# A planner that sums three engines, gate columns as steps of their own, and projection stores from ScalarE's queue

## The chip, the cores and the metric

One core of a Trainium2 chip. The kernel is a program for its engines: TensorE (PE, with its weight loads as PEld), VectorE (DVE), ScalarE (ACT), GpSimd (POOL) and SyncE (SP), each of which works through its own instruction queue in order and waits there for semaphores of the others. The metric is the device time of one execution in microseconds (us); the smaller, the better.

## The reference, cut to what matters

One layer of a transformer trunk over 1024 latent tokens and 256 context tokens, 1024 channels, float32: a SwiGLU block, then token mixing, then another SwiGLU block. The change is within token mixing.

```python
def token_mixing(h_lat, h_ctx, w_in, ...):
    p_lat = jnp.split(h_lat @ w_in, IN_SPLITS, axis=-1)   # retention q k v gate, GLA q k v gate, two low-rank gate inputs
    p_ctx = jnp.split(h_ctx @ w_in, IN_SPLITS, axis=-1)
    ret_lat = retention_inputs(p_lat, n_lat)              # q, k with rotary embedding; 4 heads of 128
    gla_lat_f, gla_lat_b = gla_inputs(p_lat, ...)         # g = log_sigmoid(p[8] @ w_f + b_f) / 16; 4 heads, dk 64, dv 128
    o_ret_l, _ = bidir_prefix(retention_chunked, ...)     # forward and backward scans over chunks of 128,
    o_gla_l, _ = bidir_prefix(gla_chunked, ...)           # and of 64, from the context's final states
    return merge_outputs(o_ret_l, o_gla_l, p_lat, ...)    # normalise, multiply by silu(gate), @ w_out
...
def gla_chunked(q, k, v, g, s0):                          # one chunk
    b = jnp.cumsum(gc, axis=-2)
    scores = jnp.einsum('bhid,bhjd,bhijd->bhij', qc, kc, jnp.exp(b_i - b_j))
    o = scores @ vc + (qc * jnp.exp(b)) @ s
    s = jnp.exp(b_last) * s + (kc * jnp.exp(b_last - b)).T @ vc
```

## The kernel before

The whole trunk is one program: the first SwiGLU block fills the first 845 us, the context's projections follow, mixing of the latent tokens (`lat_phase`) runs from about 926 to 1431 us, `mixed_in` and `mixed_out` (the product with w_out) until about 1527 us, and the second SwiGLU block to the end. Every large product is made of three float32r matmuls (`mm3`, L67 to L69): weights and activations are split into a high part (`whi`, `hh`; ScalarE, L62) and the rest (`wlo`, `hl`; VectorE or GpSimd, L63). Latent tokens come in two halves of 512, `tg` 0 and 1.

Mixing consists of projections and of lanes that use them. A projection unit (`unit`, `unit_v`, `unit_v0`) takes its weights in pieces, accumulates in a PSUM tile `psa` (four buffers) over 8 channel blocks, and ends in `put`: ScalarE copies the tile to `pv`, and the store to a DRAM buffer (`gqd`, `gkd`, `rqd`, `rkd`, `rvd`, `gvd`, `sgd`) is issued on `self.store`, which is GpSimd's queue. The lanes load from there again, on SyncE's queue. `unit_v0` makes the first GLA values and, in 32 more columns, the low-rank gate inputs of both directions; it copies those to four tiles `p89` (L1393), transposes them on PE (L1403) and copies the result to `p89T` (L1405).

The lanes are generators, each made of steps that begin with matmuls:

- `gate_lane`: for each `tg` and head, `gla_gates`: a matmul of `p89T` with the gate weights, softplus on ScalarE (`softplus`, L814 to L818), sums over pairs, fours and so on up to 128 on GpSimd (L1089), two exponentials on ScalarE (L1091, L1092), two stores. After the four heads of `tg` 0 come `decays` (L1068), tables for retention.
- `gla_lane`, one head after another: loads, and for each level hs = 1, 2, 4, 8, 16 copies to `zq`, `zk` (L1131 to L1134), products with gate factors (L1128, L1144), score matmuls (L1153); then states, outputs, norm (`pow_half`, L1047 and L1048) and `finish` (a transpose, L1033, the gate from `sgd`, the store to `mixd`).
- `ret_lane`, one head after another: rotary products (L1265 to L1267) over tiles `rope`, `rq`, `rs` of one buffer each, states, scores, norm (L1359), `finish`.
- a lane of the context's states, whose last product is L981 for retention (`ctx_ret`) and L956 for GLA (`ctx_gla`).

Only PE's instructions are put in order by hand: `lat_phase` runs inside `pe_order`, and the order in which the generators are advanced is PE's order. The other engines' orders come from the scheduler of the programming layer. `lat_phase` keeps a clock `self.now` of PE's planned time. Each step of a lane yields the time at which its inputs should be ready, its cost on PE and the names it needs; a step whose time has come is taken, otherwise a piece of projection from `lat_units` (in the order of the list `UNITS`) fills PE. Ready times come from one counter: `vec(us)` adds 1.25 times a duration to `self.dve`, the planned time of VectorE. ScalarE and GpSimd have no counter; their work is in constants such as `+ 6`.

In the profile's names, buffer numbers are left out: `psa` and `psb` are PSUM tiles of projections and of lanes, `t` and `t2` general tiles, `sc` and `L` the gates' tiles.

Of the kernel before, what the change touches and what calls it, by code (L numbers as in the profile page):

```python
# [30 lines left out]
class Trunk:  # L31
# [899 lines left out]
    def ctx_gla(self, h, pool):  # L931
# [15 lines left out]
        yield self.vec(3) + 5, 0.44, ()  # L947
# [5 lines left out]
        yield self.now + 2, 0.44, ()  # L953
# [6 lines left out]
        self.done[f"S{h}"] = self.now  # L960

    def ctx_ret(self, h, pool):
# [15 lines left out]
        yield self.vec(0.8) + 0.8, 0.9, ()  # L978
# [6 lines left out]
        self.done[f"T{h}"] = self.now  # L985
# [43 lines left out]
    def finish(self, on, tg, wcol, hb, pool):  # L1029
# [5 lines left out]
        if hb in self.gated:  # L1035
            sg = self.tile(pool, [P, 512], F32, "sg", 2)
            nc.sync.dma_start(sg, self.sgd[hb * P:(hb + 1) * P, tg * 512:(tg + 1) * 512])
            nc.vector.scalar_tensor_tensor(out=mx, in0=pt, scalar=wcol, in1=sg, op0=ALU.mult, op1=ALU.mult)
        else:
            self.late.add((hb, tg))  # L1040
            nc.scalar.activation(mx, pt, AF.Copy, scale=wcol)
        self.store.dma_start(self.mixd[hb * P:(hb + 1) * P, tg * 512:(tg + 1) * 512], mx)
# [19 lines left out]
    def decays(self, h, pool):  # L1062
# [10 lines left out]
        self.done[f"D{h}"] = self.vec(0.6) + 4  # L1073
# [22 lines left out]
    def vec(self, us):  # L1096
        self.dve = max(self.dve, self.now) + SLACK * us
        return self.dve

    def gla_lane(self, h, pool):  # L1100
# [18 lines left out]
        def copies(hs, tg):  # L1119
# [4 lines left out]
            w = 0.8  # L1124
            if hs == 1:
# [4 lines left out]
                w = 1.5  # L1130
# [4 lines left out]
            return self.vec(w) + 0.9  # L1135

        def scale(hs, tg):
# [8 lines left out]
            return self.vec(0.46) + 1.2  # L1146

        def scores(hs, tg):
# [7 lines left out]
            elif hs == 1:  # L1156
                sc[tg] = g[tg]
                nc.scalar.copy(sc[tg], ps)
            else:
                nc.vector.copy_predicated(c3(sc[tg]), self.msk[hs].unsqueeze(1).to_broadcast([P, 4, P]), c3(ps))  # L1160
                self.vec(0.75)

        yield self.now + 4, 0, ()
        at = {0: copies(1, 0)}
        scale(1, 0)
        for hs in (1, 2, 4, 8, 16):
# [7 lines left out]
            else:  # L1174
                at[0] = self.dve + 1.2
                at[1] = max(at[1], at[0])
            yield at[1], 0.9, ()
            scores(hs, 1)
        for hs in (32, 64):
# [14 lines left out]
        for tg in LATTG:  # L1194
# [4 lines left out]
            at[tg] = self.vec(1.1) + 0.8  # L1199
            kt.append(kh)  # L1200
        for tg in LATTG:
# [7 lines left out]
            at[tg] = self.now + 2.2  # L1209
# [12 lines left out]
        last = self.vec(4.9) + 1  # L1222
        ons = []
        for tg in LATTG:
# [16 lines left out]
            ons.append((self.vec(0.8) + 4.5, on))  # L1241
# [4 lines left out]
    def ret_lane(self, h, pool):  # L1246
# [7 lines left out]
        at = {}  # L1254
        for tg in LATTG:
# [3 lines left out]
            for src, out in ((self.rkd, k), (self.rqd, q)):  # L1259
                raw, sw = self.tile(pool, [P, 512], F32, "rq", 1), self.tile(pool, [P, 512], F32, "rs", 1)  # L1260
# [3 lines left out]
                t = self.tile(pool, [P, 512], F32, "qk", 4)  # L1264
                nc.vector.tensor_tensor(out=t, in0=raw, in1=rope[:, 0, :], op=ALU.mult)  # L1265
                nc.vector.tensor_tensor(out=sw, in0=sw, in1=rope[:, 1, :], op=ALU.mult)
                nc.vector.tensor_tensor(out=t, in0=t, in1=sw, op=ALU.add)  # L1267
                out.append(t)
                at[tg] = self.vec(2.1) + 4 + 3 * tg
# [7 lines left out]
        def decayed(d, tg):  # L1277
# [3 lines left out]
            return vd, self.vec(0.5) + 0.3  # L1281

        kt = []
        for tg in LATTG:
# [7 lines left out]
            at[tg] = self.now + 2  # L1292
        parts = ((0, 0), (1, 1), (0, 1), (1, 0))
        nxt = decayed(0, 0)
        for i, (d, tg) in enumerate(parts):
# [15 lines left out]
            last = self.vec(1.4)  # L1311
# [10 lines left out]
        def decay(tg, ps):  # L1322
# [7 lines left out]
            return self.vec(2.2) + 0.6, sc, qf  # L1330

        yield self.now, 0.9, ()
        ps = inner(0)
        ready, sc, qf = decay(0, ps)
        yield self.now, 0.9, ()
        ps = inner(1)
        for tg in LATTG:
# [15 lines left out]
            self.vec(1.5)  # L1353
# [7 lines left out]
            ons.append((self.vec(1) + 3 - 2 * (tg == 0), on))  # L1361
# [4 lines left out]
    def put(self, pool, ps, dst, fn=AF.Copy, scale=1.0, view=None):  # L1366
        t = self.tile(pool, [P, 512], F32, "pv", 4)
        self.nc.scalar.activation(t, ps, fn, scale=scale)
        self.store.dma_start(dst, view(t) if view else t)
# [10 lines left out]
    def unit_v0(self, pool, w, tg):  # L1380
# [6 lines left out]
        pT = self.psB()  # L1387
        if tg == 0:
            self.pt89 = self.tile(pool, [64, 512], F32, "p89T", 1)
        rs = []  # L1390
        for c in range(4):
            r = self.tile(pool, [P, 32], F32, "p89", 4)
            nc.scalar.copy(r, ps[c][:, 256:288])  # L1393
            rs.append(r)
# [524 lines left out]
```

## Time and profile before

| what | value |
|---|---|
| median of 3 runs | 2191.18 us (2186.52 to 2196.46) |
| profiled execution, its own time | 2184.12 us |
| its span, first to last instruction | 2180.9 us |
| mean granted TensorE clock | 0.989 |
| projections' stores on GpSimd's queue, 930 to 1450 us (L1369, L1400) | 56 |
| DMA to landing for them, median | 3.3 us |
| PE busy, 1000 to 1050 us, of 50 | 47.46 us |
| PE busy, 1150 to 1200 us, of 50 | 50.00 us |

A wait in the tables reads "engine, tile and line that waits <- engine, tile and line it waited for: us in total, times, longest". In a timeline, a row's first number is the start in us from the span's start, the second the duration, and square brackets hold the idle time before it and what ended it. ACTq, POOLq and SPq are the queues of those engines, where DMAs are issued. PEclk is the clock that PE was granted, as a share of full speed.

### The profile page before, as it was taken

To read this page: it belongs to the slowest core of one execution; us is meant where nothing else is said; L and a number is where in the kernel's file an instruction comes from. 1 tells how busy PE (TensorE), PEld (TensorE's weight loads), DVE (VectorE), ACT (ScalarE), POOL (GpSimd) and SP (SyncE) were. 2 spreads that over 40 slices of the span, in tenths; PEclk is the share of its full clock that TensorE was granted. 3 is DMA by queue.
4 is the path that set the end of the run, shared out by engine and by line. 5 is a ranking of instruction groups with operands and counts; after the bars stand their busy time and mean duration, and the time that the engine had idled before them with its cause. 6 is when DMAs were issued, how large, how long until landed. Compare 5 with 4: busy or idle time off the path is not lost.

```text
span 2180.9 us, 33346 instructions
## 1 busy us (share of the span) xinstructions
PE 2119.4 (97%) x11558; PEld 1817.0 (83%) x11558; DVE 1529.7 (70%) x2735; ACT 948.6 (43%) x1776; POOL 420.5 (19%) x572
## 2 busy tenths in 40 slices
PE   8999999999999999978999999999999999999998
PEld 7888888888888999966889789878878888887888
DVE  7889999756777657745666556477777666675676
ACT  4434334345544555655332432244343433434553
POOL 0101111110013662545232322100001111120000
PEclk9999999999999999989999999999999999999999
DMA  8267768569865566655462353573134444467674
GB/s 330 83 231 245 270 221 277 178 237 308 295 196 162 174 182 201 181 194 187 148 177 83 112 173 118 178 251 98 63 128 159 140 157 159 155 218 242 208 237 153
DMA packets 209529, 409.57 MB, mean 188 GB/s; under 512 B 26128, under 2 KB 48080, under 8 KB 209360
## 3 DMA queue, kind: packets, MB, share of 16 engines
q1 hardware_dynamic: 185600, 330.77, 48.3%
q0 software_dynamic: 23328, 76.55, 8.8%
q8 instruction: 90, 1.47, 0.3%
q14 instruction: 79, 0.65, 0.1%
q10 hardware_dynamic: 432, 0.13, 0.0%
HBM read 320.56 MB, written 86.79 MB: 187 GB/s over the span
## 4 chain that ended last, share of the span: by engine, by line
PE 79%; DVE 6%; issue 5%; DMA 4%; POOL 2%; ACT 2%; SPq 0%; POOLq 0%; ACTq 0%; DVEq 0%
PE psa L67 14%; PE psa L69 14%; PE psa L68 14%; PE psb L67 10%; PE psb L69 9%; PE psb L68 9%; PE psa L1421 3%; PE psb L1153 2%; DVE hl L226 1%; POOL L L1089 1%; DVE nt L220 1%; DMA qk<-sgd 1%; DMA raw<-in_w 1%; PE psb L1301 1%; POOL rr L1048 0%
## 5 line engine op out<-in xcount | busy, mean ns | idle before, releaser
L62 ACT ACTIVATE whi<-raw 128x512 fp32r<-128x512 f32 (+1 forms) x635 | 390.7, 622 | 673.2 <-PE psa L68 212.6
L63 DVE TENSOR_TENSOR wlo<-raw,whi 128x512 fp32r<-128x512 f32 (+1 forms) x533 | 368.2, 694 | 251.6 <-ACT whi L62 244.1
L67 PE MATMUL psa<-hh,whi 128*128 128x512 f32 (+1 forms) x1444 | 535.8, 371 | 2.2 <-ACT hh L62 1.1
L69 PE MATMUL psa<-hh,wlo 128*128 128x512 f32 (+1 forms) x1444 | 528.9, 366 | 3.1 <-POOL wlo L63 3.1
L68 PE MATMUL psa<-hl,whi 128*128 128x512 f32 (+1 forms) x1444 | 528.3, 366 | 1.2 <-DVE hl L63 1.2
L67 PEld LDWEIGHTS psa<-hh,whi 128*128 128x128 f32 x1444 | 275.4, 191 | 47.1 <-ACT hh L62 1.9
L69 PEld LDWEIGHTS psa<-hh,wlo 128*128 128x128 f32 x1444 | 274.2, 190 | 48.0 <-POOL wlo L63 4.1
L68 PEld LDWEIGHTS psa<-hl,whi 128*128 128x128 f32 x1444 | 275.0, 190 | 43.4 <-DVE hl L63 2.2
L67 PE MATMUL psb<-hh,whi 128*128 128x512 f32 (+1 forms) x680 | 259.6, 382 | 0.5 <-ACT whi L62 0.5
L69 PE MATMUL psb<-hh,wlo 128*128 128x512 f32 (+1 forms) x680 | 259.5, 382 | 0.6 <-DVE wlo L63 0.6
L68 PE MATMUL psb<-hl,whi 128*128 128x512 f32 (+1 forms) x680 | 259.4, 382 | 0.0
L63 POOL TENSOR_TENSOR wlo<-raw,whi 128x512 fp32r<-128x512 f32 (+1 forms) x102 | 136.8, 1359 | 204.2 <-ACT whi L62 199.2
L353 POOL DMA_DIRECT2D gd<-s x154 | 83.7, 544 | 388.7 <-DVE s L344 298.0
L69 PEld LDWEIGHTS psb<-hh,wlo 128*128 128x128 f32 x680 | 127.8, 188 | 25.7 <-DVE wlo L63 1.0
L67 PEld LDWEIGHTS psb<-hh,whi 128*128 128x128 f32 x680 | 127.8, 188 | 25.5 <-ACT whi L62 1.0
L68 PEld LDWEIGHTS psb<-hl,whi 128*128 128x128 f32 x680 | 127.8, 188 | 24.6
L1048 POOL TENSOR_TENSOR nr<-nr,mhalf 128x4 f32<-128x4 f32 (+1 forms) x11 | 10.3, 932 | 423.1 <-DVE nr L1047 413.5
L130 DVE CUSTOM_DVE_ANT_0 junk<-ada,condc,cols 128x1024 bf16<-128x1024 f32 x62 | 79.3, 1278 | 5.0 <-DMA ada<-in_adaT 4.7
L385 POOL DMA_DIRECT2D sd<-s x22 | 11.9, 541 | 359.3 <-DVE s L384 359.2
L63 DVE TENSOR_TENSOR hl<-raw,hh 128x512 fp32r<-128x512 f32 x93 | 65.3, 709 | 9.9 <-ACT hh L62 9.8
L62 ACT ACTIVATE hh<-raw 128x512 fp32r<-128x512 f32 x93 | 57.0, 620 | 12.2 <-DMA raw<-gd 9.8
L352 DVE TENSOR_TENSOR s<-s,s 128x512 f32<-128x512 f32 x88 | 59.0, 685 | 0.4
(421 smaller groups left out, 4070.2 us busy)
## 6 DMA issues: line engine op xcount, KB each, us to landing
raw<-in_w SPq DMA_DIRECT2D x374, 256.0 KB, 3.1
gd<-s POOLq DMA_DIRECT2D x154, 256.0 KB, 3.1
ada<-in_adaT SPq DMA_DIRECT2D x76, 512.0 KB, 4.4
raw<-gd SPq DMA_DIRECT2D x88, 256.0 KB, 3.2
s<-in_w SPq DMA_DIRECT2D x66, 256.0 KB, 4.7
sd<-s POOLq DMA_DIRECT2D x44, 256.0 KB, 2.8
raw<-sd SPq DMA_DIRECT2D x44, 256.0 KB, 3.0
hh<-in_w SPq DMA_DIRECT2D x44, 256.0 KB, 3.9
```

Of the source, the lines that this page charges most:

```text
L62: nc.scalar.activation(hi, src, AF.Copy)
L63: (eng or nc.vector).tensor_tensor(out=lo, in0=src, in1=hi.bitcast(F32), op=ALU.subtract)
L67: mm(ps, wa[0], xa[0], start=start, stop=False, skip_group_check=more)
L68: mm(ps, wa[0], xa[1], start=False, stop=False, skip_group_check=more)
L69: mm(ps, wa[1], xa[0], start=False, stop=stop, skip_group_check=more)
L130: nc.vector.tensor_tensor_reduce(out=self.junk, in0=t, in1=self.cs[s], scale=1.0, scalar=self.col("ada_b")[:, j:j + 1], op0=ALU.mult, op1= ...
L220: nc.vector.scalar_tensor_tensor(out=t, in0=self.x[tg][k], scalar=a[:, k:k + 1], in1=rb, op0=ALU.mult, op1=ALU.mult)
L226: self.nc.vector.scalar_tensor_tensor(out=lo, in0=t, scalar=b[:, k:k + 1], in1=hi.bitcast(F32), op0=ALU.add, op1=ALU.subtract)
L352: sub = lambda o, a, b: nc.vector.tensor_tensor(out=o, in0=a, in1=b, op=ALU.subtract)
L353: put = lambda i, t: self.store.dma_start(self.gd[i, f // 2], t)
L1153: nc.tensor.matmul(ps[:, s], kl[:, s], ql[:, s], start=True, stop=True)
L1421: mm(o, x[p], y[q], start=k == 0 and n == 0 and c % 2 == 0, stop=k == KD - 1 and n == 2, skip_group_check=True)
```

## The change

1. `vec` and its one counter become `w(eng, us, after)` with three: `self.clk` holds planned times of VectorE (v), ScalarE (a) and GpSimd (p), with factors 1.2, 1.1 and 1.15; every ready time gets 0.7 us (`LAG`) on top. The lanes' steps charge what they put on each engine. Weight loads charge ScalarE 0.63 and VectorE 0.69 each, for the split.
2. The transposes of the low-rank columns and the copy to `p89T` move from `unit_v0` to `gate_lane`, as a step for each `tg` (L1062 and L1064 in the new numbering). The gates' steps are no longer ready all at once but one after another by ScalarE's counter, and `decays` come after both halves' gates, one step for each head.
3. `put` and `unit_v0` issue their 56 stores on ScalarE's queue (L1396 and L1426) instead of GpSimd's.
4. `rq` and `rs` get two buffers each.
5. `UNITS`: the key, query and value projections of retention heads 2 and 3 come earlier, the retention gates rg0 and rg1 later.

```diff
+    def w(self, eng, us, after=0):
+        c = max(self.clk[eng], self.now)
+        self.clk[eng] = c + SLACK[eng] * us
+        return max(c, after) + SLACK[eng] * us + 0.15
-    def vec(self, us):
-        self.dve = max(self.dve, self.now) + SLACK * us
-        return self.dve
...
     def gate_lane(self, pool):
         nc = self.nc
+        self.pt89 = self.tile(pool, [64, 512], F32, "p89T", 1)
         for tg in LATTG:
             yield 0, 0, (("ga0", "gv0")[tg],)
+            yield self.w("a", 0.8), 0.4, ()
+            pT = self.psB()
+            for c in range(4):
+                nc.tensor.transpose(pT[:32, c * P:(c + 1) * P], self.r89[c], self.ident)
+            self.p89T[tg] = self.pt89[32 * tg:32 * tg + 32]
+            nc.scalar.copy(self.p89T[tg], pT[:32])
+            at = self.w("a", 0.6)
             for h in range(4):
-                yield self.now, 0.45, ()
+                yield at, 0.45, ()
                 self.gla_gates(h, tg, pool)
-                self.done[f"G{tg}{h}"] = self.vec(1.4) + 6
-            if tg == 0:
-                for h in range(4):
-                    self.decays(h, pool)
+                t = self.w("v", 1.43, self.w("a", 1.9))
+                t = self.w("a", 1.25, self.w("p", 3.2, t))
+                at = self.clk["a"] - 2.5
+                self.done[f"G{tg}{h}"] = self.w("p", 1.2, t)
+        for h in range(4):
+            yield self.clk["a"], 0, ()
+            self.decays(h, pool)
+            self.done[f"D{h}"] = self.w("p", 0.6, self.w("v", 0.6, self.w("a", 1.6)))
...
             for src, out in ((self.rkd, k), (self.rqd, q)):
-                raw, sw = self.tile(pool, [P, 512], F32, "rq", 1), self.tile(pool, [P, 512], F32, "rs", 1)
+                raw, sw = self.tile(pool, [P, 512], F32, "rq", 2), self.tile(pool, [P, 512], F32, "rs", 2)
...
-            ons.append((self.vec(0.8) + 4.5, on))
+            t = self.w("v", 0.2, self.w("v", 0.7, self.w("a", 0.62)))
+            ons.append((self.w("a", 1.15, self.w("p", 1.3, t)), on))
...
     def put(self, pool, ps, dst, fn=AF.Copy, scale=1.0, view=None):
         t = self.tile(pool, [P, 512], F32, "pv", 4)
         self.nc.scalar.activation(t, ps, fn, scale=scale)
-        self.store.dma_start(dst, view(t) if view else t)
+        self.nc.scalar.dma_start(dst, view(t) if view else t)
+        self.w("a", 1.0)
...
         for c in range(2):
             r0 = 512 * tg + 256 * c
-            self.store.dma_start(self.gvd[r0:r0 + 256, :256].rearrange("(c p) e -> p c e", p=P), t[c].rearrange("p (c e) -> p c e", c=2))
-        yield KD, None, 0.5
-        for c in range(4):
-            nc.tensor.transpose(pT[:32, c * P:(c + 1) * P], rs[c], self.ident)
-        self.p89T[tg] = self.pt89[32 * tg:32 * tg + 32]
-        nc.scalar.copy(self.p89T[tg], pT[:32])
+            nc.scalar.dma_start(self.gvd[r0:r0 + 256, :256].rearrange("(c p) e -> p c e", p=P), t[c].rearrange("p (c e) -> p c e", c=2))
...
                 u[2].append(self.load_half(s))
+                self.w("a", 0.63), self.w("v", 0.69)
...
-                lane[1:] = y
+                lane[1:] = [y[0] + LAG, *y[1:]]
...
-UNITS = ("gv0", "gk0", "gq0", "rk0", "rq0", "rv0", "rk1", "rq1", "gk1", "gq1", "gv1", "gg0", "rg0", "gg1", "rk2", "rq2", "rv1",
-         "rg1", "rk3", "rq3", "gg2", "rg2", "gg3", "rg3")
+UNITS = ("gv0", "gk0", "gq0", "rk0", "rq0", "rv0", "rk1", "rq1", "gk1", "gq1", "gv1", "gg0", "rk2", "rq2", "rv1", "rg0", "gg1",
+         "rk3", "rq3", "rg1", "gg2", "rg2", "gg3", "rg3")
```

What it moves, at three places. First PE, at the end of the second half of gv0 (matmuls of 128x288), before: the four transposes follow at once, then the first projection of gk0 (`hh_2061`).

```order
L67 MATMUL psa_10172<-whi_10257,hh_1333_5979 128x288
L68 MATMUL psa_10172<-wlo_10258,hh_1333_5979 128x288
L69 MATMUL psa_10172<-whi_10257,hl_1334_5980 128x288
L1403 MATMUL psb_10484<-ident_82,p_2369_10485 32x128
L1403 MATMUL psb_10484<-ident_82,p_2370_10487 32x128
L1403 MATMUL psb_10484<-ident_82,p_2371_10489 32x128
L1403 MATMUL psb_10484<-ident_82,p_2372_10491 32x128
L67 MATMUL psa_10506<-hh_2061_9175,whi_10422 128x512
```

And after: the first projection follows at once; it takes the PSUM buffer that psa_10163 held.

```order
L68 MATMUL psa_10165<-wlo_10252,hh_1333_5979 128x288
L69 MATMUL psa_10165<-whi_10251,hl_1334_5980 128x288
L67 MATMUL psa_10166<-whi_10251,hh_1333_5979 128x288
L68 MATMUL psa_10166<-wlo_10252,hh_1333_5979 128x288
L69 MATMUL psa_10166<-whi_10251,hl_1334_5980 128x288
L67 MATMUL psa_10412<-hh_2061_9175,whi_10269 128x512
L68 MATMUL psa_10412<-hl_2062_9176,whi_10269 128x512
```

The transposes now stand 77 rows further on, between two projections:

```order
L68 MATMUL psa_10548<-hl_2076_9190,whi_10415 128x512
L69 MATMUL psa_10548<-hh_2075_9189,wlo_10416 128x512
L1062 MATMUL psb_10599<-ident_82,p_2352_10396 32x128
L1062 MATMUL psb_10599<-ident_82,p_2353_10398 32x128
L1062 MATMUL psb_10599<-ident_82,p_2354_10400 32x128
L1062 MATMUL psb_10599<-ident_82,p_2355_10402 32x128
L67 MATMUL psa_10598<-hh_1319_5965,whi_10346 128x512
L68 MATMUL psa_10598<-hl_1320_5966,whi_10346 128x512
```

ScalarE at the same place, before: the exponentials of the first half's gates (`sc`, `L`) and the decay tables (`dec`, `t` from `tab`) stand ahead of the copies of the low-rank columns (`p`) and of the values (`pv`) of the second half.

```order
L1092 ACTIVATE L_10320<-L_10320 128x508
L1091 ACTIVATE sc_10354<-sc_10354 128x512
L1068 ACTIVATE dec_10378<-tab_9877,lgx_9879 128x128 x3
L972 COPY t_2360_10429<-psb_10426 128x256
L1393 COPY p_2369_10485<-psa_10169 128x32
L1393 COPY p_2370_10487<-psa_10170 128x32
L1393 COPY p_2371_10489<-psa_10171 128x32
L1393 COPY p_2372_10491<-psa_10172 128x32
L1397 COPY pv_10493<-psa_10169 128x256
L1397 COPY pv_10493<-psa_10170 128x256
L1397 COPY pv_10494<-psa_10171 128x256
```

And after, with what each row waits for (DMAHW are completion semaphores that SyncE's loads use too): gates 0 and 1 stand among the copies, the decay tables are gone, and the first of gv0's stores is issued here.

```order
L1106 ACTIVATE sc_10318<-sc_10318 128x512 [waits Pool_49]
L817 ACTIVATE t_2349_10361<-t_2349_10361 128x512 [waits Activation_49]
L1418 COPY p_2353_10398<-psa_10164 128x32
L1418 COPY p_2354_10400<-psa_10165 128x32
L818 ACTIVATE t_2349_10361<-t_2349_10361 128x512 [waits Activation_49]
L1107 ACTIVATE L_10307<-L_10307 128x508 [waits Pool_49]
L1418 COPY p_2355_10402<-psa_10166 128x32
L1422 COPY pv_10404<-psa_10163 128x256
L1422 COPY pv_10404<-psa_10164 128x256
L1422 COPY pv_10405<-psa_10165 128x256
L1422 COPY pv_10405<-psa_10166 128x256
L1426 DMA gvd<-pv_10404 128x2x256 [waits DMAHW1_49,Activation_49]
```

Only one gate's last exponential (L1107) is left ahead of the value copies that free the projections' PSUM buffers.

VectorE in the GLA lane's last head before, where the second half's first level is made (`zq_2249`, `zk_2250`): the rotary product of retention's third head is in front, on its second rope tile.

```order
L63 TENSOR_TENSOR wlo_13807<-raw_13804,whi_13806 128x512
L1133 COPY zk_2250_9955<-B_2859_13516 64x256
L1265 TENSOR_TENSOR qk_13663<-rq_13656,rope_13654 128x512
L1128 TENSOR_TENSOR A_2858_13515<-A_2858_13515,sc_13511 64x512
L1131 COPY zq_2249_9954<-A_2858_13515 64x256
L1144 TENSOR_TENSOR A_2858_13515<-A_2858_13515,sc_13511 128x256
L1266 TENSOR_TENSOR rs_13657<-rs_13657,rope_13654 128x512
```

After, at the same point of the GLA lane's third head, the rotary product reads retention's first rope tile of that head:

```order
L1149 COPY zk_2250_9955<-B_2777_12931 64x256
L1288 TENSOR_TENSOR qk_13250<-rq_13243,rope_13241 128x512
L1144 TENSOR_TENSOR A_2776_12930<-A_2776_12930,sc_12926 64x512
L1147 COPY zq_2249_9954<-A_2776_12930 64x256
L63 TENSOR_TENSOR wlo_13176<-raw_13173,whi_13175 128x512
```

And for the second head, retention's second rope tile is read between the first level and the next:

```order
L1147 COPY zq_2249_9954<-A_2635_11986 64x256
L1288 TENSOR_TENSOR qk_12063<-rq_12056,rope_12054 128x512
L1161 TENSOR_TENSOR A_2635_11986<-A_2635_11986,sc_11982 128x256
L1149 COPY zk_2254_9963<-B_2636_11987 64x64x4
L1147 COPY zq_2251_9958<-A_2635_11986 64x128x2
```

The row moved from one level's copies to another's, and from the fourth head to the second and third.

More of the change, by code (lines that the diff above doesn't have):

```diff
@@ L952, in ctx_gla @@
         nc.scalar.copy(kt[:, :n], pt[:, :n])
-        yield self.now + 2, 0.44, ()
+        yield self.w("a", 0.4), 0.44, ()
         ps = self.psB()
@@ L1208, in gla_lane @@
             nc.scalar.copy(A[tg][b], B[tg][b])
-            at[tg] = self.now + 2.2
+            at[tg] = self.w("a", 0.62)
+            self.w("a", 0.4)
         for tg in LATTG:
@@ L1254, in ret_lane @@
         at = {}
+        tq = self.now + 4.5
         for tg in LATTG:
@@ L1291, in ret_lane @@
             kt.append(t)
-            at[tg] = self.now + 2
+            at[tg] = self.w("a", 0.62)
         parts = ((0, 0), (1, 1), (0, 1), (1, 0))
@@ L1329, in decay @@
             nc.vector.tensor_tensor(out=c3(sc), in0=c3(ps), in1=dec[:, 0:1, :].to_broadcast([P, 4, P]), op=ALU.mult)
-            return self.vec(2.2) + 0.6, sc, qf
-        yield self.now, 0.9, ()
+            return self.w("v", 2.25, max(last, q_at)), sc, qf
+        q_at = tq - 0.5
+        yield q_at - 3, 0.9, ()
         ps = inner(0)
         ready, sc, qf = decay(0, ps)
-        yield self.now, 0.9, ()
+        yield q_at, 0.9, ()
         ps = inner(1)
```

72 lines of the change are left out of this document (40 added, 32 removed).

## The prediction

> **What bounds the kernel now.** I read the page first: busy shares, granted clock.
>
> ```profile
> PE 2119.4 (97%) x11558; PEld 1817.0 (83%) x11558; DVE 1529.7 (70%) x2735; ACT 948.6 (43%) x1776; POOL 420.5 (19%) x572
> PEclk9999999999999999989999999999999999999999
> ```
>
> TensorE (PE) is the bound, and nearly full over the span. The change touches only mixing, 930 to 1450 us, so I then asked for the busy time there, stretch by stretch (columns: stretch, length, busy of each engine, granted clock, DMA).
>
> ```profile
> 930.00:1000.00 70.00, 53.45 (x264) 42.50 (x263) 34.77 (x89) 43.93 (x105) 36.08 (x81) 0.87 0.59 197
> ...
> 1200.00:1250.00 50.00, 47.13 (x328) 39.86 (x328) 24.48 (x48) 22.63 (x50) 17.67 (x24) 0.97 0.35 115
> 1250.00:1300.00 50.00, 45.02 (x281) 40.34 (x277) 27.30 (x60) 20.93 (x46) 14.87 (x18) 0.93 0.58 177
> ...
> sum 597.00, PE 563.20 PEld 487.36 DVE 353.52 ACT 244.75 POOL 156.01; mean PE 51.20 PEld 44.30 DVE 32.14 ACT 22.25 POOL 14.18
> ```
>
> PE is idle for 597.0 - 563.2 = 33.8 us between 930 and 1527, half of it before 1000 (70.00 - 53.45 = 16.6). Which waits these are is in PE's wait table of 930 to 1480:
>
> ```profile
> PE psb L1403 <- ACT p L1393: 12.0, 2, 11.5
> PE psb L1153 <- DVE zq L1131: 4.5, 1, 4.5
> PE psb L981 <- ACT t L818: 3.9, 1, 3.9
> PE psb L1033 <- ACT t L1240: 3.8, 3, 2.9
> PE psb L1033 <- DVE t2r L1359: 2.1, 2, 1.5
> PE psb L950 <- DVE t L946: 1.9, 1, 1.9
> PE psb L1214 <- ACT t L1207: 1.4, 2, 1.0
> ...
> PE psa L67 <- ACT hh L62: 0.7, 1, 0.7
> ```
>
> Four waits make up most of it. Each also costs afterwards: PE windows cut at the stalls show the clock.
>
> ```profile
> 971.30:975.10 3.80, 3.77 (x11) 0.50 0.59 243
> ...
> 996.20:1000.20 4.00, 3.99 (x9) 0.50 0.65 221
> 1000.20:1005.00 4.80, 4.80 (x18) 0.76 0.82 259
> ...
> 1208.00:1214.00 6.00, 6.00 (x22) 0.78 0.34 134
> ...
> 1293.40:1300.00 6.60, 6.60 (x33) 0.54 0.60 197
> ```
>
> Time lost to the lower clock is length x (1 - clock): 1.9 us after the first stall, 2.0 + 1.2 after the one at 996, 1.3 after 1207, 3.0 after 1293: 9.4 in all. So the most that any order could win in this stage is 33.8 + 9.4 = 43 us, 2% of the span.
>
> **The change, part by part.**
>
> *Low-rank transposes and gates as steps of their own.* Why the 11.5 us exist is in ScalarE's timeline:
>
> ```profile
> 950.07 0.69 ACT L814 ACTIVATE t<-psb,cols 128x512 f32<-128x512 f32 x1
> ...
> 957.74 0.63 ACT L1092 ACTIVATE L<-L 128x508 f32<-128x508 f32 x1 [1.72 <-POOL L L1089]
> ...
> 963.06 0.63 ACT L1092 ACTIVATE L<-L 128x508 f32<-128x508 f32 x1 [1.71 <-POOL L L1089]
> ...
> 968.87 0.63 ACT L1092 ACTIVATE L<-L 128x508 f32<-128x508 f32 x1 [1.19 <-POOL L L1089]
> ...
> 971.09 0.44 ACT L1393 COPY p<-psa 128x32 f32<-128x32 f32 x4
> 971.40 0.95 ACT L1397 COPY pv<-psa 128x256 f32<-128x256 f32 x3
> ```
>
> ```profile
> 959.49 0.29 PE L69 MATMUL psa<-whi,hl 128*128 128x288 f32 x1
> 971.33 1.03 PE L1403 MATMUL psb<-ident,p 128*32 128x128 f32 x4 [11.54 <-ACT p L1393]
> ```
>
> PE ends the second half of gv0 and wants its four low-rank copies at once; ScalarE serves in order and has the first half's four gates in front, whose L1092 wait each time for GpSimd's running sums. Changed, PE has other matmuls where the transposes stood, and one whole gate, no longer three and more, is ahead of the copies. It does not go to nothing: the next matmul of a projection needs the PSUM tile that these copies release, and ScalarE has L1107 (the former L1092) of gate 0 in front of it. One gate takes ScalarE from 950.07 to 957.74 + 0.63, some 8 us; the gate's matmul now stands 24 matmuls of 0.13 us (the spacing at 959) before the piece's end, 3.1 us. So 8 - 3 = 5 us stay, 6.5 of 11.5 are won. Bounds: 0 (three gates still ahead in effect) and 11.5. I count no clock gain there: 5 us idle is more than the 2.9 us at 1207 that already lowered the clock.
>
> On that clock the Trainium skill, page "TensorE: Matmul & The Clock Gate", section "HAM oscillation — how this bites in real kernels", says that only idle gaps above about 3.4 us let the clock fall. Here the 0.78 after a wait of 2.87 us differs from it; by the page the stall at 1207 costs 1.3 us less and the sum below is about 1 us smaller. I go by the row.
>
> *The context key states (L981, at 996).* Its PE wait of 3.9 plus 3.2 of clock, 7.1 us, comes from a key copy (L972) that ScalarE reaches only behind two L1092 of the second half's gates, in the same way. With gates spaced, one is ahead: I take 5 of 7.1 (bounds 0 and 7.1). A cost comes with it: the first of these products now comes earlier, behind a split of a weight that has only just landed at 946.4,
>
> ```profile
> 946.38 0.63 ACT L62 ACTIVATE whi<-raw 128x512 fp32r<-128x512 f32 x1 [1.99 <-DMA raw<-in_wgk]
> 949.28 0.63 ACT L62 ACTIVATE whi<-raw 128x512 fp32r<-128x512 f32 x1 [2.26 <-DMA raw<-in_wgk]
> ```
>
> and I charge 2.5 us, about one such wait. Net 2.5.
>
> *Rotary rows (1293).* PE waited for zq, and VectorE had stood at the rotary product:
>
> ```profile
> 1291.63 0.69 DVE L1265 TENSOR_TENSOR qk<-rq,rope 128x512 f32<-128x512 f32 x1 [4.68 <-DMA rope<-in_rope]
> 1292.24 0.68 DVE L1128 TENSOR_TENSOR A<-A,sc 64x512 f32<-64x512 f32 x1
> 1292.95 0.28 DVE L1131 COPY zq<-A 64x256 f32<-64x256 f32 x1
> ```
>
> 4.5 + 3.0 of clock. rq and rs get a second buffer, rope does not. In the new order the product that stands like this one, right ahead of GLA head 2's second-half copies, reads a rope tile whose load is issued long before; but for head 1 the second rope tile, reloaded into the one buffer, is read ahead of the next level's copies (the order of VectorE shows it). Of 7.5 I take 4 (bounds 0, 7.5).
>
> *L1033 behind L1240 (1207)*: 2.9 + 1.3 of clock; the GpSimd power of the norm is now in the plan (1.3 us) and the finish stands later. I take 2.5 of 4.2. *L1033 behind L1359* (2.1 in two): 1. *The end*: behind the last finish there now stand some 17 us of projection matmuls before w_out, where it was the last thing, so w_out's first splits,
>
> ```profile
> 1436.71 0.50 PE L67 MATMUL psa<-hh,whi 128*128 128x512 f32 x1 [0.72 <-ACT hh L62]
> 1437.85 0.50 PE L68 MATMUL psa<-hl,whi 128*128 128x512 f32 x1 [0.64 <-DVE hl L63]
> ```
>
> lose 1.4, of which I take 1. The L950 and L1214 rows (3.3) keep their causes: 0.
>
> *Stores from ScalarE's queue.* 52 stores of put and 4 of unit_v0 leave GpSimd:
>
> ```profile
> L1369 POOL DMA_DIRECT2D sgd<-pv x16: 540/581/597, 1213.9 to 1431.3; - x16
> L1369 POOL DMA_DIRECT2D rvd<-pv x8: 725/733/765, 1065.4 to 1313.7; - x8
> L1400 POOL DMA_DIRECT2D gvd<-pv x4: 715/737/782, 939.8 to 974.8; - x4
> ```
>
> ```profile
> 1.16 0.46 ACTq L76 DMA_DIRECT2D ccol<-in_ccol  x1
> ```
>
> GpSimd gives up 40 x 0.58 + 16 x 0.74 = 35 us of issuing, and stops holding its sums and rr behind a late copy. It is 19% busy and the terms above hold what PE saw of it, so further gain 0 (bounds 0 and 35). ScalarE, 244.75 of 597 us busy here, gains 56 x 0.45 = 25 us, and each store now stands in front of the next split or copy. In the order's waits it also takes turns with SyncE's loads on the same eight completion semaphores (DMAHW0 to 7), so a store can wait in ScalarE's queue for an older load, and a load for an older store. Bounds: 0 (all under ScalarE's idle) to 25 for the issues alone. In PE's table the longest wait for a projection (psa) is 0.7 us, so I am near the lower end: 3 us, one issue in eight. The Trainium skill, page "DMA: Bandwidth & Descriptors", section "Issuing engines are not separate DMA queues", speaks against any gain here: the transfers run on the same 16 DMA engines whoever issues them, and only the issuing sequencer's time is saved. By it alone this part is 0 or a loss, as I have it; no row of before shows a data store issued by ScalarE.
>
> *Decay tables after both gate halves, UNITS' new order, loads charged in the plan*: the same instructions (PE has the same number); ScalarE's L1068 leave the place before the copies, which is in the first term. Retention heads 1 to 3 start earlier, and GLA units later: hidden under fill, 0.
>
> Sum: 6.5 + 2.5 + 4 + 2.5 + 1 + 1 - 3 = 14.5 us. The profiled execution took 2184.1 (span 2180.9 and 3.2 around it), 7 below the median 2191.2 of the runs; against it the change gives 2169.6, and against the median 2191.2 - 14.5 = 2177.
>
> **Rivals.** (a) *The waits move*: PE has still eight gates to pass, each 8 us on ScalarE with two waits for GpSimd, and projections need ScalarE's copies between. If each gate costs PE 1.5 us through a PSUM tile that is released late, 12 us come back: 2189. For it: GpSimd's sums are no faster. Against it: 12 to 24 projection matmuls stand between two gates now, where four gates stood next to each other. (b) *ScalarE's queue becomes the bound* (slower): stores wait there for loads' semaphores, splits come late, PE waits on whi. A store's landing took 3.3 us in the median:
>
> ```profile
> DMA to landing us min/median/max: 2.3/3.3/6.3
> ```
>
> If PE loses 0.31 us for each of the 56, the gain of 17.5 is gone, and from there it is slower; at 0.6, 34 us, the kernel is at 2191 + 34 - 17.5 = 2207. For it, SyncE is often held, and a load that is late then holds a store, and the splits behind the store:
>
> ```profile
> SPq L264 <- DVE wlo L63: 102.2, 27, 11.3
> ```
>
> Against it, ScalarE is idle over half of the stage. (c) *Most of the stalls go*: 43 less 8 that keep their causes: 35 us, 2156. For it: every large wait has an edit aimed at its queue; against it: the 5 us worked out above.
>
> **How the numbers follow.** 0.5% is 11 us, about what a measurement of this kernel tells from no change. The forecast, terms partly won: 0.52, its own range 2166 to 2185, of which 0.39 lies below 2180 and 0.13 above. (c) 0.13, all faster. (a) 0.20: 0.02 faster, 0.17 same, 0.01 slower. (b) 0.15: 0.03 same, 0.12 slower. Together faster 0.54, same 0.33, slower 0.13. The range leaves out the far half of (c) and of (b): 2154 to 2198.
>
> **What would show it.** L1062 (the former L1403) without a wait above 1 us; one wait of about 5 us at 955 to 962 on an L67 of psa released by ACT pv, half clock after it; L982 once at 2 to 3 us near 946; no wait of 4 us near 1290; GpSimd with 56 instructions fewer; PE idle over 930 to 1527 near 20 us rather than 34. Wrong it is if PE's table gets rows of psa for ACT whi or pv above 5 us together, if ScalarE's stores wait for semaphores of loads, or if rope's wait comes back at another head with the same 4 us.

## The result, and the profile after

The changed kernel takes 2163.7 us (2162.2 to 2166.0), the kernel before 2189.2 in the same comparison: ratio 0.9879, 95% interval [0.9852, 0.9906], some 26 us faster. The direction and the stage of the forecast held, and so did the mechanism for PE's order; its size did not, 14.5 us against about 26, and one term, the stores, had the wrong sign. Both profiled executions lie at the low end of their kernel's runs, before's further than after's: they are 22 us apart (2184.1 and 2162.2), and the readings below explain those 22.

The gain is all in mixing. From the first 288-column matmul to the norm behind w_out, PE windows of before and of after, in this order (stretch, length, PE busy, granted clock, DMA):

```profile
898.10:1481.80 583.70, 548.09 (x3631) 0.97 0.51 163
```

```profile
900.50:1460.50 560.00, 539.12 (x3632) 0.99 0.53 170
```

583.7 has become 560.0 us, 23.7 less, with the same matmuls. The code ahead of this stretch and behind it is the same; it took 2.4 and 0.8 us longer in this execution of after. Idle time fell from 35.6 to 20.9, which is 14.7 of the 23.7. The other 9.0 are busy time, most of it slow matmuls that are gone. PE windows over the stretches in which the clock was at half, before and then after:

```profile
951.30:954.70 3.40, 3.40 (x14) 0.50 0.38 128
964.90:975.20 10.30, 3.87 (x12) 0.50 0.43 175
995.60:1002.50 6.90, 6.29 (x14) 0.51 0.61 207
1132.20:1135.60 3.40, 3.40 (x9) 0.50 1.04 321
1207.30:1210.70 3.40, 3.40 (x10) 0.50 0.21 78
1292.60:1299.40 6.80, 6.02 (x29) 0.50 0.56 186
```

```profile
963.30:970.20 6.90, 4.23 (x10) 0.51 0.53 190
1035.00:1038.40 3.40, 3.40 (x18) 0.50 0.72 224
1284.20:1287.60 3.40, 3.40 (x14) 0.50 0.19 77
```

PE was busy at half clock for 26.4 us before and for 11.0 after; half of each is lost, 13.2 and 5.5, so 7.7 of the 9.0 are the clock's. It added half as much again to the idle time that was won.

PE's waits of after, 920 to 1480 us:

```profile
PE psa L67 <- ACT pv L1422: 6.4, 3, 5.1
PE psb L1034 <- ACT t L1261: 4.2, 2, 3.5
PE psa L1442 <- ACT pv L1395: 2.0, 1, 2.0
PE psb L1171 <- DVE zk L1149: 1.7, 1, 1.7
PE psa L68 <- DVE hl L63: 1.4, 1, 1.4
```

No row is left of the transposes, of the context's states (L982, the former L981), of zq behind VectorE, or of L1386 (the former L1359). The one wait that the forecast kept is there, 5.09 us against 5 worked out. ScalarE's timeline has gate 0's last exponential ahead of the copies, PE's has the wait, and PE's windows show the slow clock behind it and behind the wait of 3.5 us at 1283:

```profile
964.94 0.63 ACT L1107 ACTIVATE L<-L 128x508 f32<-128x508 f32 x1 [1.55 <-POOL L L1104]
965.47 0.17 ACT L1418 COPY p<-psa 128x32 f32<-128x32 f32 x1
965.54 0.93 ACT L1422 COPY pv<-psa 128x256 f32<-128x256 f32 x3
```

```profile
965.97 0.80 PE L67 MATMUL psa<-hh,whi 128*128 128x512 f32 x1 [5.09 <-ACT pv L1422]
```

```profile
965.95:969.80 3.85, 3.83 (x9) 0.50 0.37 140
...
1283.60:1287.20 3.60, 3.57 (x16) 0.58 0.18 73
```

The stores' issues on ScalarE's queue (duration in ns, least, median, most), and their landing:

```profile
L1396 ACTq DMA_DIRECT2D sgd<-pv x16: 326/327/345, 1199.8 to 1411.0; - x16
L1396 ACTq DMA_DIRECT2D rvd<-pv x8: 366/372/412, 1056.9 to 1257.8; - x8
```

```profile
DMA to landing us min/median/max: 2.0/2.7/7.8
```

An issue takes ScalarE 0.33 us where GpSimd took 0.58, and the store lands 2.7 us after it in the median, in place of 3.3.

### The profile page after: what moved, and what is told of

The parts are those of the page before. It is cut to its first block, busy times and chain, and to the rows that moved or that the text cites. A ratio compares the mean times of both kernels' runs of the same rounds, so it can differ in the third digit from the quotient of the medians.

```text
span 2160.4 us, 33264 instructions
## 1 busy us (share of the span) xinstructions
PE 2112.7 (98%) x11558; PEld 1811.5 (84%) x11558; DVE 1527.3 (71%) x2735; ACT 950.2 (44%) x1777; POOL 386.8 (18%) x516
## 4 chain that ended last, share of the span: by engine, by line
PE 84%; DVE 5%; issue 4%; DMA 3%; POOL 2%; ACT 1%; SPq 0%; ACTq 0%; POOLq 0%; DVEq 0%
PE psa L67 15%; PE psa L69 15%; PE psa L68 15%; PE psb L67 10%; PE psb L69 10%; PE psb L68 10%; PE psa L1442 3%; PE psb L1171 2%; DVE hl L226 1%; DVE nt L220 1%; DMA raw<-in_w 1%; POOL L L1104 1%; PE psb L1327 1%; PE psb L1371 1%; DVE wlo L63 1%
```

## Experiments

Each run was timed beside the kernel before, and ratios are to it. Changes of 0.3% between two runs are about what their intervals can separate. Where a difference is given "by the medians", the two runs' median times are subtracted instead; the two ways differ by some us.

**1. The stores back on GpSimd's queue, all else as changed (e1).** PE's order is identical. That of ScalarE and VectorE is not: the scheduler of the programming layer makes it, and places some of their rows elsewhere when the stores move.

```diff
-        self.nc.scalar.dma_start(dst, view(t) if view else t)
+        self.store.dma_start(dst, view(t) if view else t)
...      # the same for the two stores of unit_v0
```

> The changed kernel with its 56 projection stores issued on GpSimd's queue again; PE's order is the same. Theory O (the gain is PE's order: gates as steps, three counters): the stores' queue is worth 0 to -3 us, so 2160 to 2164, ratio 0.986 to 0.988. Rival Q (the gain that was not counted comes from GpSimd, which issues 35 us less and so sums and norms earlier): 7 us or more come back, 2171, ratio 0.991, with a wait for L1107 or for a norm's power back in PE's table.

Measured: 2172.8, ratio 0.9945 [0.9931, 0.9958]. Against the change's 0.9879 the queue is worth 0.66%, 14 us (8 to 21 with the two intervals; 9 by the medians). The order alone gains 0.55%, 12 us (15 by the medians). So Theory O is refuted on the stores and Rival Q holds: they are a third to a half of the whole gain.

The trace shows places where it goes. The profiled executions are 15 us apart in span, and some 4.4 of them have another cause, a wait of 2.7 us for L982 at 954 and half clock for 3.4 us behind it: a weight's load landed late there, and GpSimd had no row from 945.8 to 956.4.

```profile
952.82 0.63 ACT L62 ACTIVATE whi<-raw 128x512 fp32r<-128x512 f32 x1 [4.55 <-DMA raw<-in_wgk]
```

The queue shows at the fourth gate. GpSimd and ScalarE in e1, and the same sums in the changed kernel:

```profile
982.60 0.56 POOL L1396 DMA_DIRECT2D gkd<-pv  x1 [0.28 <-issue]
...
989.83 0.41 ACT L1150 COPY zk<-A 64x256 f32<-64x256 f32 x1 [2.86 <-DMA A<-gkd]
990.27 0.63 ACT L817 ACTIVATE t<-t 128x512 f32<-128x512 f32 x1
...
992.83 0.54 POOL L1396 DMA_DIRECT2D gkd<-pv  x1 [6.47 <-ACT pv L1395]
993.39 0.62 POOL L1104 TENSOR_TENSOR L<-sc 128x256 f32<-128x256 f32 x1
```

```profile
984.64 0.61 POOL L1104 TENSOR_TENSOR L<-sc 128x256 f32<-128x256 f32 x1 [4.63 <-DVE sc L1100]
```

The first store leaves 1.2 us after its copy, behind two sums. ScalarE waits 2.86 us for those keys to be loaded again, in the middle of the fourth gate (L817 is that gate's), and the sums then stand behind the second store, which waits for its copy. The gate's matmul on PE is 5.0 us later than in the changed kernel (985.1 against 980.1), its sums are 8.7. Is it the queue, or that ScalarE has the copy of keys ahead of L817 here and behind L818 in the changed kernel? The run of experiment 7 with the stores on SyncE's queue (e12) has ScalarE's rows of this gate, L814 and on, in e1's order, and the copy waits for nothing:

```profile
982.62 0.42 ACT L1150 COPY zk<-A 64x256 f32<-64x256 f32 x1
```

Its sums begin at 985.6, 1.0 us later than in the changed kernel, where its PE is 0.6 later. So at this gate the queue costs some 3.3 us and ScalarE's order 0.4. GpSimd around 1030 us in e1:

```profile
1027.10 0.54 POOL L1396 DMA_DIRECT2D rkd<-pv  x1
1029.30 0.61 POOL L1104 TENSOR_TENSOR L<-sc 128x256 f32<-128x256 f32 x1 [1.66 <-DVE sc L1100]
1029.98 2.64 POOL L1104 TENSOR_TENSOR L<-L 128x128 f32<-128x128 f32 x5
...
1033.41 0.21 POOL L1104 TENSOR_TENSOR L<-L 128x4 f32<-128x4 f32 x1
1033.70 1.26 POOL L1145 TENSOR_TENSOR B<-B,sc 64x512 f32<-64x512 f32 x1
```

and PE behind it:

```profile
1035.46 1.16 PE L1171 MATMUL psb<-zq,zk 128*128 128x128 f32 x8 [3.15 <-ACT zq L1148]
```

Sums, stores, decay tables and the GLA lane's first product (L1145) share one in-order queue, and the late gate makes all of them late. In the changed kernel the same product starts at 1024.67, and the same matmul waits 0.90 us:

```profile
1024.67 1.76 POOL L1145 TENSOR_TENSOR B<-B,sc 64x512 f32<-64x512 f32 x1
```

```profile
1026.94 1.16 PE L1171 MATMUL psb<-zq,zk 128*128 128x128 f32 x8 [0.90 <-ACT zq L1148]
```

**2. A load on either queue (e9, e10).** Behind each store on ScalarE a small DMA is issued, once on GpSimd's queue, once on ScalarE's.

```diff
         self.nc.scalar.dma_start(dst, view(t) if view else t)
+        self.store.dma_start(self.tinyd[self.ntiny], t[:, :16])     # e9; e10: self.nc.scalar
+        self.ntiny += 1
...      # the same in unit_v0
```

> The changed kernel, in which every one of the 56 projection stores on ScalarE's queue is followed by a small DMA (128 rows of 64 bytes of the same tile, to a buffer that nobody reads) on GpSimd's queue. Theory R (the 9 us of e1 are GpSimd's in-order queue: a store waits there for its copy and then takes 0.6 us, in front of the gates' sums and the GLA products): most of it returns, 2169 to 2173. Rival L (the 9 us came from how soon the stores themselves land): GpSimd's rows cost nothing, 2163 to 2166.

> The changed kernel with the same 56 small DMAs, but on ScalarE's queue behind each store: it doubles what the change costs ScalarE. If an issue costs PE one eighth of its 0.45 us (my 3 us): 2166 to 2168. If ScalarE hides it: 2163 to 2165. If its queue is near the bound: 2170 or more with PE waits for ACT pv or whi.

Measured: e9 2170.1, 0.9913 [0.9899, 0.9927]; e10 2160.2, 0.9864 [0.9847, 0.9882]. On GpSimd the 56 rows bring back 6 us by the medians and 7 by the ratios (1 to 14 with the two intervals), although the stores proper still leave from ScalarE and land nearly as early (2.9 us after their issue in the median, against 2.7). The same DMAs on ScalarE's queue bring back nothing, so it is not the transfers: it is the place in GpSimd's queue that costs, Theory R. Idle time of GpSimd just before the small DMAs, which wait there for their copies (what ended it, us, times):

```profile
  ACT pv L1395: 106.5, 37
```

The first matmul of the second half's scores, in e9 and then in e10, with GpSimd's product L1145 at the same place in its order in both:

```profile
1028.19 1.16 PE L1171 MATMUL psb<-zq,zk 128*128 128x128 f32 x8 [3.27 <-ACT zq L1148]
```

```profile
1026.48 1.16 PE L1171 MATMUL psb<-zq,zk 128*128 128x128 f32 x8 [0.89 <-ACT zq L1148]
```

On ScalarE twice as many issues show no cost (0.15% faster than the change, with intervals from 10 us faster to 4 slower). So the sum's price of 3 us for 56 of them was too high as far as this shows, and an issue took 0.33 us there, where the sum had 0.45.

**3. The queue alone, in the old order (e3).**

```diff
 # kernel before
-        self.store.dma_start(dst, view(t) if view else t)
+        self.nc.scalar.dma_start(dst, view(t) if view else t)
...      # the same in unit_v0
```

> The kernel before with the 56 stores on ScalarE's queue, nothing else; PE's order is that of before. Theory O: ScalarE pays, 2189 to 2193, ratio 1.000 to 1.002. Rival Q: GpSimd's relief shows here too, 2180 or less, ratio 0.996, PE's wait of 11.5 us at 971 shorter by 2 us or more.

Measured: 2186.7, 0.9996 [0.9985, 1.0006]: the queue is worth nothing there (3 us at most by the interval). The large waits of the old order are not GpSimd's to shorten; PE's table of e3 still has them (10.7 for 11.5, 4.4 for 4.5):

```profile
PE psb L1403 <- ACT p L1393: 12.8, 2, 10.7
PE psb L1153 <- DVE zq L1131: 4.4, 1, 4.4
```

**4. What the queue's worth needs (e8, e13).** The gates of a half ready at once, with the stores on ScalarE (e8) and on GpSimd (e13).

```diff
-                yield at, 0.45, ()
+                yield self.now, 0.45, ()
                 self.gla_gates(h, tg, pool)
```

> The changed kernel with the gates of a half ready at once (each step yields the current time, as before), the transposes and the decays as changed. Theory G (spacing the gates by ScalarE's counter is what brings the gain at 960 to 1000): 5 us or more lost, 2169 or more, with PE waits for pv or t copies of ScalarE of 8 us together between 955 and 1005. Rival: 2163 to 2166, the spacing does nothing that the step and the decays' new place do not.

> The gates at once (as e8_gates_at_once, 2172.9) and the projection stores on GpSimd as well: what the queue is worth without the spacing. Theory I (the queue's worth needs the spaced gates, since only then do sums, stores and the GLA lane's first products alternate on GpSimd): it is worth 3 us or less here, 2173 to 2176. Rival A (its worth is the same 9 us wherever PE has few other waits): 2180 to 2184.

Measured: e8 2172.9, 0.9926 [0.9912, 0.9940]; e13 2177.5, 0.9938 [0.9918, 0.9958]. Spacing is worth 0.47%, 10 us (4 to 17 with the intervals); Theory G holds. Without it the queue is worth 0.12%, 3 us (4.5 by the medians; from 3 the other way to 8 with the intervals), less than with it. That is for Theory I, though 2177.5 lies between the two ranges. With gates in a block something else is late. PE's waits of e8 have it at the context's keys and again at pv:

```profile
PE psa L67 <- ACT pv L1422: 5.4, 2, 4.1
PE psb L971 <- DMA t<-crk: 4.5, 1, 4.5
```

**5. The step of its own (e4, e5).** e4 moves the transposes into such a step in the kernel before and changes nothing else; e5 moves them back in the changed one.

```diff
 # e4: kernel before, gate_lane
             yield 0, 0, (("ga0", "gv0")[tg],)
+            yield self.now, 0.4, ()
+            pT = self.psB()
+            for c in range(4):
+                nc.tensor.transpose(pT[:32, c * P:(c + 1) * P], self.r89[c], self.ident)
+            self.p89T[tg] = self.pt89[32 * tg:32 * tg + 32]
+            nc.scalar.copy(self.p89T[tg], pT[:32])
...   # and the same rows out of unit_v0
```

> The kernel before with the low-rank transposes as a step of the gate lane, everything else (one counter, gates all ready at once, stores on GpSimd) as before. Theory O in its weak form (moving the transposes alone takes the wait at 971 off PE's path): 6 us or more gained, 2183, ratio 0.997. Rival P (four gates still stand ahead of the copies in ScalarE's queue, and PE then waits for the PSUM buffer instead of the transposes): the 11 us stay as a wait of psa for ACT pv, 2187 to 2191, ratio 0.999 to 1.001.

> The changed kernel with the low-rank transposes back in unit_v0 (as before), all else as changed: three counters, spaced gates, stores on ScalarE. Theory C (the counters and the spacing carry the gain, the step of its own is small): 2164 to 2170, with a wait of the transposes for ACT p of 2 to 5 us. Rival S (the step is needed, the order of the transposes makes the wait): 2175 or more, a wait of 8 us or more at the transposes.

Measured: e4 2199.4, 1.0068 [1.0055, 1.0082], slower than either theory had it; e5 2167.6, 0.9903 [0.9886, 0.9920]. Under the old counter the step is harmful: PE still waits 9.7 us, for the PSUM tile in place of the transposes (Rival P), and new waits join, with a mean clock of 0.984.

```profile
PE psa L67 <- ACT pv L1401: 9.9, 2, 9.7
PE psb L1033 <- ACT t L1247: 5.4, 3, 3.2
PE psb L950 <- DVE t L946: 4.3, 1, 4.3
PE psb L1088 <- ACT p89T L1060: 3.8, 2, 3.1
```

With the new counters the step is worth 0.24%, which these intervals do not separate from nothing. Theory C holds so far: with the step small, the list and the buffers too (experiment 6) and the spacing worth 10 us, the counters and the spacing are what is left to carry the order's gain. No run has the counters alone.

**6. Buffers and the list of units (e2, e6).** e2 has one buffer each for rq and rs, e6 the old list as well.

```diff
-                raw, sw = self.tile(pool, [P, 512], F32, "rq", 2), self.tile(pool, [P, 512], F32, "rs", 2)
+                raw, sw = self.tile(pool, [P, 512], F32, "rq", 1), self.tile(pool, [P, 512], F32, "rs", 1)
 # e6 besides: UNITS as before
```

> The changed kernel with one buffer each for rq and rs again; PE's order is the same. Theory O: 0 to 2 us, 2164 to 2166. Rival B (the rotary wait of 7.5 us with its slow clock went because the second buffer let rows load earlier): a wait of some 4 us for a rotary row at zq or at a retention score comes back, 2169 to 2171, ratio 0.991.

> The changed kernel with the old list UNITS, and with one buffer for rq and rs (with two it does not fit). To be read beside e2_one_buffer, 2165.3. Theory C: the list is worth 0 to 3 us, so 2165 to 2168. Rival U (the rotary wait went because retention's keys and queries were projected earlier): 2171 or more, with a VectorE wait for rope or rq of 4 us and a PE wait behind it.

Measured: e2 2165.3, 0.9912 [0.9898, 0.9927]; e6 2167.0, 0.9896 [0.9883, 0.9910]. e6 differs from e2 by less than the intervals, and e2 from the change by 1.6 us in the medians (0.33% by the ratios, at the edge of what the intervals separate). In neither is there a PE wait for zq above 1.1 us, or for zk above 2.2. So the rotary wait at 1293 did not go through buffers (Rival B) or the list (Rival U), and the order of the lanes is what is left.

**7. The stores on SyncE, and the gates' stores on ScalarE too (e12, e11).**

```diff
 # e12
-        self.nc.scalar.dma_start(dst, view(t) if view else t)
+        self.nc.sync.dma_start(dst, view(t) if view else t)
...      # the same in unit_v0
 # e11
-        self.store.dma_start(self.ggd[h, tg], g)
-        self.store.dma_start(self.gLd[h, tg][:, :508], L[:, :508])
+        nc.scalar.dma_start(self.ggd[h, tg], g)
+        nc.scalar.dma_start(self.gLd[h, tg][:, :508], L[:, :508])
```

> The changed kernel with the 56 projection stores on SyncE's queue: neither GpSimd nor ScalarE issues them. Theory R: GpSimd stays free and ScalarE gets 25 us back: 2160 to 2164, if SyncE's loads behind a store that waits for its copy are early enough. Rival H (SyncE's in-order queue is held by stores, loads come late): 2168 or more, with ACT or DVE waits for DMA raw, rope or rq that grow by 10 us.

> The changed kernel with the 16 stores of the gates (ggd, gLd) issued on ScalarE too, right behind the exponentials that make them, instead of on GpSimd between the sums. Theory R: 16 x 0.55 = 9 us less on GpSimd just where it is busiest, 950 to 1050: 2 to 4 us gained, 2160 to 2162. Rival (ScalarE is as tight there): 2164 to 2167.

Measured: e12 2166.8, 0.9896 [0.9882, 0.9909], between both theories: most of the gain is there with GpSimd free, whichever other queue takes the stores. e12 also tells something of what the scheduler's other order is worth in e1. Its PE order and the order of GpSimd's products and sums are e1's, and around 1010 to 1030 ScalarE has the gates' rows in e1's order, not in the changed kernel's. It is 3 us slower than the change by the medians, and 6 faster than e1 (0.49% by the ratios, 11 us, 7 to 15 with the intervals). So most of the queue's worth is GpSimd's queue itself, as e9 has it too. PE's wait for zq at 1029 is 2.7 us in e12 as well, with no such store on GpSimd: that wait, which e1 has at 1035, can also come from ScalarE's order.

e11 2164.7, 0.9890 [0.9877, 0.9904]: no gain. Either GpSimd's remaining rows there no longer decide, or ScalarE pays as much as they did; the run does not part the two.

**8. The wait that was left (e7, e14).** e7 begins the first half's gates after both halves of gv0; e14 moves unit_v0's copies from ScalarE to VectorE.

```diff
 # e7, gate_lane
             at = self.w("a", 0.6)
+            yield at, 0, ("gv0",)
+            at = max(at, self.now)
 # e14, unit_v0, and the same for the pv copies
-            nc.scalar.copy(r, ps[c][:, 256:288])
+            nc.vector.tensor_copy(r, ps[c][:, 256:288])
```

> The changed kernel, but the first half's gates begin only when both halves of gv0 are planned, so that no gate stands ahead of the second half's copies. If the wait of 5.1 us for those copies and the clock after it are all that gate 0 costs: 2163.7 - 7 = 2157. Rival D (the gates are the start of a chain to the GLA lane, which begins some 6 us later, and its waits come at other places): 2161 to 2168.

> The changed kernel with the copies of unit_v0 (low-rank columns and values) on VectorE instead of ScalarE, so that they no longer stand behind gate 0's last exponential, which waits for GpSimd. If that queue position is all of the wait of 5.1 us at 966 and its slow clock: 2156 to 2158. Rival D (the wait moves on, as in e7): 2161 to 2165. If VectorE's own work is held by these copies: 2166 or more.

Measured: e7 2162.6, 0.9872 [0.9858, 0.9887], as the change; e14 2173.3, 0.9925 [0.9910, 0.9941], 10 us slower. In both the wait of 5.1 is gone and others stand elsewhere; for e7 that is

```profile
PE psa L1444 <- ACT pv L1397: 4.2, 1, 4.2
```

and for e14

```profile
PE psb L951 <- DVE t L946: 6.9, 2, 4.8
PE psa L67 <- DVE pv L1422: 4.8, 2, 2.6
```

Of all that ran, none is faster than the changed kernel beyond the intervals.

## Why the prediction was right in kind and short in size

*The first wait* (6.5 forecast): right, for the reason given; 11.54 us became 5.09, and the clock after it is the same 0.50: 6.4. That it came out so close is partly luck. The gate took ScalarE 9.5 us (956.08 to 965.57) where the working had 8, since the next gate's rows stand between its own, and its matmul stood 4.8 us before the piece's end (956.0 to 960.9) where the working had 3.1, since the next gate's matmuls stand there too. The two errors cancel.

*The context's states* (net 2.5): the 7.1 us of wait and clock are gone, all of them; the charge of 2.5 for a late split was too high, since no L982 wait of 0.4 us or more stands in the table. Gain 7.1, less 1.3 for the other two waits of pv L1422 (6.4 - 5.1). In e1 the charged wait does appear, 2.7 us behind L977, with the weight that landed late in front of it as the working had it: it was a real risk. It is not the stores' doing.

```profile
PE psb L982 <- DVE t L977: 2.7, 1, 2.7
```

*Rotary rows* (4 of 7.5): the old wait and its slow clock, 7.5, are gone. The row that the working feared, a rotary product on the second rope tile ahead of the next level's copies, does hold them up, but by little; PE's new wait for zk stands behind it and is counted below.

```profile
1045.84 0.69 DVE L1288 TENSOR_TENSOR qk<-rq,rope 128x512 f32<-128x512 f32 x1 [0.63 <-DMA rope<-in_rope]
```

```profile
1047.68 1.13 PE L1171 MATMUL psb<-zq,zk 128*128 128x128 f32 x8 [1.74 <-DVE zk L1149]
```

*L1033 behind the norm* (2.5 gained): wrong, it moved. It waits 3.5 us at 1283 and loses 3.6 x 0.42 = 1.5 to the clock, 5.0 in place of 4.2, so -0.8.

*L1359* (1): its 2.1 us of wait and the slow matmuls behind it are gone; PE now is busy for all of 1120 to 1140 (20.00 of 20), against 17.78 at 0.91 before. That is 2.2 idle and 1.8 of clock, 4. *L950 and L1214* (0): their 3.3 us went, and two new waits, L1442 and zk, cost 3.7. *The end* (1): 1.4 before, 1.4 after, 0.

Sum: 6.4 + 5.8 + 7.5 - 0.8 + 4 - 0.4 = 22.5, near the 23.7 of the stage. It leaves out two stretches of half clock of 1.7 us each, 951.3 to 954.7 in before, which is gone, and 1035.0 to 1038.4 in after, which is new; they cancel. The prediction's 9.4 us for the clock missed that first one and the one at 1132.2. It is 13.2, and the most that an order could win was 47 us, not 43.

The failed step is *"Stores from ScalarE's queue"*, taken as -3: "the terms above hold what PE saw of it, so further gain 0". GpSimd's share of 19% over the span, and PE's table of the old order, said nothing about what GpSimd would hold up once the large waits in front were gone. As measured (e1 against the change) the term is +9 to +14; e9 (against the change) and e12 (against e1) put some 6 of the 9 on the place in GpSimd's queue, and e10 shows no price on ScalarE. How much of the rest is the order that the scheduler gives ScalarE and VectorE stays open. Part of the terms above is this one under another name: in e1 PE's waits for zq and zk are 6.8 us in place of 2.6, the one for zk behind the rotary row, which there waits 2.52 us for rope. The order's worth, 12 to 15, is below the 17.5 that the sum had for it. The sign by which the prediction would be wrong, psa rows for ACT pv above 5 us together, did show (6.4 and 2.0), though 5.1 of it is the wait that it forecast itself. Rival (b) did not come: behind the copies of put (L1395) PE waits 2.0 us in all, and no row for a weight's split is longer than 1.2. Rival (c) came in part, by a way it did not name.

On the clock, the Trainium skill, "TensorE: Matmul & The Clock Gate", section "HAM oscillation — how this bites in real kernels", has idle gaps above some 3.4 us lower it. The waits of 5.09 and 3.5 us agree: half clock stands behind each. Two stretches of 3.4 us do not, the one at 1207 in before, behind a wait of 2.87, and the one at 1035 in after, where no wait in the 20 us before it was longer than 2.0. On the queue, the Trainium skill, "DMA: Bandwidth & Descriptors", section "Issuing engines are not separate DMA queues", grants another issuing engine only its sequencer's time, usually small beside the DMA. An issue of 0.58 us beside a landing of 3.3 agrees with that; the 9 us of e1 are not issue time alone, since the work behind the DMA in the same queue waits with it for the copy.

## What to carry to other kernels

A store on an engine's in-order queue waits there for its producer, and everything behind it waits too (GpSimd sat idle 106.5 us before the small DMAs of e9); the engine's busy share does not show it, so look at what stands behind each DMA and who needs it, in the order that will run, not in the one that is being replaced. Parts of a change to an order are not additive: the queue was worth nothing before, 3 us with gates in a block and 9 to 14 with gates spaced, and the step alone cost 12 to 15 us. Where a scheduler orders the other engines, an edit of one queue also moves rows in theirs. Price a stall with the clock after it: behind waits of 2.9 to 5.1 us another 1.7 to 3.1 us were lost in slow matmuls.

## What the runs showed of the hardware

A second DMA behind each of the 56 stores on ScalarE's queue showed no cost (0.9864 against 0.9879), the same DMA on GpSimd's 6 to 7 us (0.9913). A store of 256 KB took 0.33 us to issue on ScalarE and 0.58 on GpSimd. A PE wait of 3.5 us was followed by 3.6 us at a clock of 0.58, one of 5.09 by 3.9 us at 0.50, and the 11.54 of before by 3.8 us at 0.50. The loss behind a stall, taken as half of PE's busy time in the windows at half clock, did not follow its length: 1.7 us behind 2.87 and behind 3.5, 1.9 behind 11.54 and 2.1 behind 5.09, but 3.1 behind 3.9 and 3.0 behind 4.5. In the windows in the section on the result the clock of mixing was at half for 3.4 us or about two or three times that, so a value such as 0.58 is the mean over a window that holds full and half clock.
